# Row norms, rotary angles and adaLN sums in the first stage of a hybrid decoder block: other engines, another order

## The chip, the cores and the metric

One core of one Trainium2 chip runs the kernel, in float32. The core has TensorE (PE, matrix products into PSUM), VectorE (DVE), ScalarE (ACT, activation tables) and GpSimd (POOL), and a queue on SyncE (SP) that issues all the DMAs here. Each engine works through its own list of instructions in order and waits on semaphores for the others. The metric is the device time of one execution in microseconds, the median of several.

## The reference, cut to what matters

One decoder layer, 1024 positions of width 1024. Token mixing (two kinds of attention), then an MLP, each ahead with a modulated RMS norm. What the change touches is the norm ahead of the first projection, its modulation, and the rotary angles:

```python
def rms_norm(x, g):
    return x * rsqrt(mean(x * x, axis=-1, keepdims=True) + EPS) * g

ang = positions[..., None] * inv_freq            # 8 frequencies
cos, sin = jnp.cos(ang), jnp.sin(ang)
mod = silu(c) @ w_ada + b_ada                    # 6 vectors of 1024
sh_a, sc_a, gt_a, sh_m, sc_m, gt_m = split(mod, 6)
h = rms_norm(x, g_attn_pre) * (1 + sc_a) + sh_a
proj = h @ w_in                                  # 1024 x 2304, then attention
```

Behind it: rotary rotation of parts of `proj`, banded and dilated attention, an output projection, and `square(relu(h @ w_up)) @ w_down`.

## The kernel before, in words

A planner written in Python (class `Sched`) decides at build time in which order each engine gets its instructions. Every piece of work is an `op` with an engine (or a choice of engines), an estimated duration, what it depends on, buffers it takes and gives, a priority `prio` (lower goes first) and an urgency `crit`: `pick` takes the operation that can start first, unless one of higher `crit` can start within half its duration. What comes out is a fixed list for each engine; the estimates play no part when the kernel runs.

The first stage, up to some 60 us, computes `h` transposed and starts the first projection unit:

- x comes in eight blocks of 128 rows, `x_t[0]` to `x_t[7]`, in two halves of four. `x_block` squares and sums a block (`junk`, result in `ssq`; ScalarE L656 or VectorE L660), `rsqrt_mean` makes `rstd` of it (GpSimd: L484 adds EPS, L486 is a power of -0.5), and the block is scaled in place (`x_sb`; L676 on ScalarE, L677 on VectorE).
- `f_cond` makes silu(c) (`cond`) and a diagonal matrix of it (`diag`, L603). Two products with ones spread it over all partitions (`condb`, L614).
- `ada_chunk(k)`, for chunk k of 8 (128 channels each), has two sums over a tile `wa` of w_ada times `condb`, the scale `g_a` and the shift `s_a` (L687, a custom VectorE instruction with a read of its accumulator), and a small product (L691).
- `mod_chunk(k, half)`: four transposes into PSUM (`pxt`, L706), which need all four scaled blocks of the half; then ScalarE applies scale and shift twice, rounded to `hw` (L708, the high part) and whole to `h` (L714), and VectorE takes the difference as the low part (L717).
- `split_w` makes a high part (L560) and a low part (L565) of each piece of w_in. A product is then three matmuls, L909, L910 (high part of h) and L912 (low part).
- While TensorE has nothing to do, `filler` puts products of ones in its list (L926), up to the first product that uses the filler's own PSUM bank.
- The rotary angle is a product of position and frequency, brought into range by 2 x 2 rounding steps (L632, L633) and 12 parts of 2 pi that are subtracted (L635), then four closing steps (L639 to L642): 26 VectorE instructions of 128x64 (one of them L628), in groups of five, in `turn_steps`. Then two sines on ScalarE (`f_sin`, L649, L650), a negation (L731), and on GpSimd two sets of ten copies into rows (`tables`, L741, L747), which TensorE transposes (`ptab`, L753).

All loads go through SP in one order: x blocks 0 to 3, two tiles of w_ada, a piece of w_in, x blocks 4 to 7, then the rest in turn.

Of the kernel before, what the change touches and what calls it, by code (L numbers as in the profile page):

```python
# [189 lines left out]
class Sched:  # L190
# [162 lines left out]
def t_dv(n):  # L353
    return 0.066 + 0.00104 * n
# [19 lines left out]
def hybrid_block(ctx: ExitStack, tc: tile.TileContext, x, positions, w_mod, w_ada, b_ada, g_attn_post, w_in, w_out,  # L374
# [3 lines left out]
    V, A, G, T = nc.vector, nc.scalar, nc.gpsimd, nc.tensor  # L378
# [45 lines left out]
    ones = const.tile([P, P], F32, name="ones")  # L424
    nhalf = const.tile([P, KC], F32, name="nhalf")
# [10 lines left out]
    ssq = const.tile([P, TB], F32, name="ssq")  # L436
    rstd = const.tile([P, TB], F32, name="rstd")
# [18 lines left out]
    p0 = pool("p0", 1, "right", stack=right0)  # L456
# [20 lines left out]
    POOL_D1, POOL_D2 = (0.25, 0.65), (0.5, 1.2)  # L477

    def rsqrt_mean(dst, src, deps, dur):
        box, n = [], dst.shape[-1]  # L480

        def first():
            box.append(small.tile([P, 8], F32, name="rs_t", tag="rs_t"))
            G.tensor_scalar(box[0][:, 0:n], src, EPS, None, ALU.add)  # L484
        e = op("POOL", dur[0], first, deps, prio=0)
        return op("POOL", dur[1], lambda: G.tensor_tensor(dst, box[0][:, 0:n], nhalf[:, 0:n], ALU.pow), [e], prio=0)  # L486
# [7 lines left out]
    posf = p0.tile([P, TB], F32, name="posf")  # L494
# [9 lines left out]
    def r_in(a):  # L504
        return r_stg if a in beside else r_wa
# [20 lines left out]
    wa_t, wa_e = {}, {}  # L526
# [11 lines left out]
    x_t, x_e = {}, {}  # L538
# [55 lines left out]

    e_sin = op("ACT", 1.5, lambda: A.activation(small.tile([P, 8], F32, name="rs_t", tag="rs_t")[:, 0:1], ones[:, 0:1],
                                                AF.Sin), [e, e_init], prio=0)
# [9 lines left out]
    e = e_cond = op("DVE", 0.52 + t_dv(D), f_cond, [e], takes=[(r_wa, 1)], prio=0)  # L606
    e_condb = []
# [9 lines left out]
    def f_cols():  # L617
# [10 lines left out]
    turn_steps = [(0.22, lambda: V.tensor_tensor(ang[:], posf[:].unsqueeze(2).to_broadcast([P, TB, 8]),  # L628
                                                 inv_f.unsqueeze(1).to_broadcast([P, TB, 8]), ALU.mult))]

    def turns(inv, parts):
        turn_steps.append((0.2, lambda: V.tensor_scalar(kq[:], ang[:], inv, ROUND, ALU.mult, ALU.add)))  # L632
        turn_steps.append((0.2, lambda: V.tensor_scalar(kq[:], kq[:], -ROUND, None, ALU.add)))  # L633
        for part in parts:
            turn_steps.append((0.26, lambda part=part: V.scalar_tensor_tensor(ang[:], kq[:], -part, ang[:], ALU.mult,  # L635
                                                                              ALU.add)))
    turns(1.0 / (TWO_PI * 4096), COARSE)
    turns(1.0 / TWO_PI, FINE)
    turn_steps += [(0.2, lambda: V.tensor_scalar(ang[:], ang[:], 3.1415925, -3.1415925, ALU.min, ALU.max)),  # L639
                   (0.2, lambda: V.tensor_scalar(kq[:], ang[:], -1.0, None, ALU.mult)),  # L640
                   (0.22, lambda: V.tensor_tensor(kq[:], kq[:], ang[:], ALU.max)),
                   (0.2, lambda: V.tensor_scalar(kq[:], kq[:], -1.0, float(np.pi / 2), ALU.mult, ALU.add))]  # L642
# [8 lines left out]
    e_ang, e_xn = e, [[], []]  # L651

    def x_block(tb):
        def f_sq():
            junk = p0.tile([P, D], BF16, name="junk", tag="junk", bufs=2)
            A.activation(junk[:], x_t[tb][:], AF.Square, scale=1.0 / 32, accum_out=ssq[:, tb:tb + 1])  # L656

        def f_sq2():
            junk = p0.tile([P, D], BF16, name="junk", tag="junk", bufs=2)
            V.tensor_tensor_reduce(junk[:], x_t[tb][:], x_t[tb][:], 1.0 / D, 0.0, ALU.mult, ALU.add, ssq[:, tb:tb + 1])  # L660
        half = tb // 4
        e = op(("ACT", "DVE"), (1.25, 1.4), (f_sq, f_sq2), [x_e[tb]], prio=1 if half else -1)
        if half:
            pair.append((tb, e))
            if len(pair) < 2 and tb < 6:
                return
            tbs = [t for t, _ in pair]
            e = rsqrt_mean(rstd[:, tbs[0]:tbs[-1] + 1], ssq[:, tbs[0]:tbs[-1] + 1], [z for _, z in pair],
                           POOL_D2 if len(pair) > 1 else (0.3, 0.9))
            pair.clear()  # L670
        else:
            tbs = [tb]
            e = rsqrt_mean(rstd[:, tb:tb + 1], ssq[:, tb:tb + 1], [e], POOL_D1)
        for t in tbs:
            e_xn[half].append(op(("ACT", "DVE"), (1.15, 0.76),
                                 (lambda t=t: A.mul(x_t[t][:], x_t[t][:], rstd[:, t:t + 1]),  # L676
                                  lambda t=t: V.tensor_scalar(x_t[t][:], x_t[t][:], rstd[:, t:t + 1], None, ALU.mult)),  # L677
                                 [e], prio=-1))
    pair = []

    e_hh, e_hl, e_ada = {}, {}, {}

    def ada_chunk(k):

        def dot(i, dst):
            w = wa_t[k, i][:]
            V.tensor_tensor_reduce(w, w, condb[:], 1.0, bb[:, k, i:i + 1], ALU.mult, ALU.add, dst[:, k:k + 1])  # L687

        def f_g():
            dot(1, g_a)  # L690
            V.tensor_tensor(g_a[:, k:k + 1], g_a[:, k:k + 1], cols[:, 8 + k:9 + k], ALU.mult)  # L691
# [1742 lines left out]
```

## Time and profile before

| | us |
|---|---|
| median of three runs | 1099.63 (1098.22 to 2195.83) |
| the profiled execution's own time | 1098.02 |
| its span, first to last instruction | 1096.2 |
| mean granted TensorE clock in it | 0.998 |

"Span" is what the rows of the timeline are counted in; what lies around it is 1.8 us here. In a row of the timeline stand the start, the duration, the engine with the line, what is written and read, the shape, and in brackets how long the engine had been idle and who released it. A row of the stretches gives for each engine the busy time and the number of instructions; then the granted clock, the share of the DMA engines and GB/s. Rows of groups give a count, the sum and the mean in ns.

### The profile page before, as it was taken

How to read it: one execution, taken by the hardware profiler on the slowest of the kernel's cores; microseconds unless marked ns; L12 is line 12 of the kernel's file. 1: busy time of each engine (PE TensorE's matmuls, PEld its weight loads, DVE VectorE, ACT ScalarE, POOL GpSimd, SP SyncE). 2: the span in 40 equal slices, each digit the busy share in tenths (PEclk: the TensorE clock that was granted, in tenths of full speed). 3: DMA queues.
4: the chain of work that ended last, by engine and by line, in shares of the span. 5: the costliest groups of instructions: out<-in, count | busy, mean ns of one | idle time of the engine just before them, and what ended most of it. 6: DMA issues, size and time to landing. Idle time of an engine off the chain costs nothing.

```text
span 1096.2 us, 15266 instructions
## 1 busy us (share of the span) xinstructions
PE 1077.7 (98%) x5254; PEld 899.0 (82%) x5254; DVE 811.2 (74%) x1434; ACT 621.7 (57%) x1155; POOL 285.0 (26%) x378
## 2 busy tenths in 40 slices
PE   8999999999999999999999999999999999999996
PEld 6888888888888888888888888888888888888885
DVE  7968776766768687699796654897645995537998
ACT  6868876555556867686755244732245632337442
POOL 4649778596846531100000000000000000000002
PEclk9999999999999999999999999999999999999999
DMA  8565656454635457368711579231575043583104
GB/s 339 212 207 161 194 168 216 140 187 141 202 106 174 135 151 264 114 230 321 280 70 39 188 256 353 77 111 62 208 284 190 1 134 140 191 324 132 58 1 154
DMA packets 87230, 189.55 MB, mean 173 GB/s; under 512 B 8304, under 2 KB 24816, under 8 KB 87152
## 3 DMA queue, kind: packets, MB, share of 16 engines
q1 hardware_dynamic: 87152, 188.56, 49.6%
q8 instruction: 42, 0.69, 0.2%
q14 instruction: 36, 0.29, 0.1%
HBM read 139.25 MB, written 30.41 MB: 155 GB/s over the span
## 4 chain that ended last, share of the span: by engine, by line
PE 92%; DVE 4%; issue 1%; POOL 1%; ACT 1%; DMA 0%; DVEq 0%; POOLq 0%; SPq 0%
PE mlp_ps L2252 18%; PE mlp_ps L2250 18%; PE mlp_ps L2251 18%; PE pj L909 5%; PE pj L912 5%; PE pj L910 5%; PE y_ps L1815 3%; PE y_ps L1817 3%; PE y_ps L1816 3%; PE o_ps L1514 2%; PE s_ps L1323 1%; PE s_ps L1228 1%; PE o_ps L1415 1%; PE pt_ps L1380 1%; PE pt_ps L1479 1%
## 5 line engine op out<-in xcount | busy, mean ns | idle before, releaser
L2250 PE MATMUL mlp_ps<-hw 128*128 128x512 f32 x896 | 349.6, 390 | 0.0
L2252 PE MATMUL mlp_ps<-hw 128*128 128x512 f32 x896 | 348.6, 389 | 0.0
L2251 PE MATMUL mlp_ps<-hw 128*128 128x512 f32 x896 | 348.6, 389 | 0.0
L2251 PEld LDWEIGHTS mlp_ps<-hw 128*128 128x128 f32 x896 | 168.2, 188 | 35.3 <-issue 0.5
L2250 PEld LDWEIGHTS mlp_ps<-hw 128*128 128x128 f32 x896 | 168.2, 188 | 35.3 <-issue 0.5
L2252 PEld LDWEIGHTS mlp_ps<-hw 128*128 128x128 f32 x896 | 168.2, 188 | 34.9
L2017 DVE TENSOR_TENSOR hw<-w,hw 128x1024 fp32r<-128x1024 f32 x94 | 112.2, 1221 | 95.7 <-ACT hw L2010 93.0
L2010 ACT CAST hw<-w 128x1024 fp32r<-128x1024 f32 x94 | 95.7, 1050 | 129.8 <-PE mlp_ps L2252 94.5
L2350 POOL TENSOR_TENSOR st<-st,nhalf 128x1 f32<-128x1 f32 x8 | 7.8, 983 | 612.7 <-DVE st L2348 612.7
L909 PE MATMUL pj<-hw,w_hl 128*128 128x512 f32 x240 | 101.8, 424 | 0.0
L912 PE MATMUL pj<-hw,w_hl 128*128 128x512 f32 x240 | 94.5, 394 | 0.0
L910 PE MATMUL pj<-hw,w_hl 128*128 128x512 f32 x240 | 94.2, 392 | 0.0
L2010 ACT CAST hw<-u 128x1024 fp32r<-128x1024 f32 x48 | 48.7, 1053 | 64.5 <-PE mlp_ps L2252 64.5
L2017 DVE TENSOR_TENSOR hw<-u,hw 128x1024 fp32r<-128x1024 f32 x48 | 57.0, 1220 | 18.1 <-ACT hw L2010 18.1
L2308 DVE TENSOR_TENSOR yacc<-yacc,mlp_ps 128x512 f32<-128x512 f32 x96 | 62.2, 683 | 3.3 <-PE mlp_ps L2252 3.3
L1062 POOL TENSOR_TENSOR ada_acc<-ada_acc,wa_st 128x512 f32<-128x512 f32 x42 | 56.1, 1336 | 3.5
L912 PEld LDWEIGHTS pj<-hw,w_hl 128*128 128x128 f32 x240 | 45.0, 188 | 10.2
L1815 PE MATMUL y_ps<-hw,oh 128*128 128x512 f32 x128 | 51.6, 403 | 0.0
L1816 PE MATMUL y_ps<-hw,oh 128*128 128x512 f32 x128 | 50.0, 391 | 0.0
L909 PEld LDWEIGHTS pj<-hw,w_hl 128*128 128x128 f32 x240 | 45.4, 189 | 4.6
L910 PEld LDWEIGHTS pj<-hw,w_hl 128*128 128x128 f32 x240 | 45.5, 190 | 4.4
L2289 ACT ACTIVATE u<-u 128x512 f32<-128x512 f32 x48 | 29.0, 625 | 30.7 <-DVE u L2287 30.1
(259 smaller groups left out, 1988.3 us busy)
## 6 DMA issues: line engine op xcount, KB each, us to landing
hw<-s_dram SPq DMA_DIRECT2D x84, 512.0 KB, 4.1
wa_st<-in_w_ada SPq DMA_DIRECT2D x32, 512.0 KB, 4.5
w<-in_w_up SPq DMA_DIRECT2D x32, 512.0 KB, 4.7
w<-in_w_down SPq DMA_DIRECT2D x32, 512.0 KB, 6.8
s_dram<-hw SPq DMA_DIRECT2D x28, 512.0 KB, 3.2
qt<-hl SPq DMA_DIRECT2D x40, 256.0 KB, 2.5
w_st<-in_w_in SPq DMA_DIRECT2D x36, 256.0 KB, 3.0
x_sb<-in_x SPq DMA_DIRECT2D x16, 512.0 KB, 6.0
```

Of the source, the lines that this page charges most:

```text
L909: T.matmul(ps, w[:, 0, n], h[0], start=(k == 0), stop=False)
L910: T.matmul(ps, w[:, 1, n], h[0], start=False, stop=False)
L912: T.matmul(ps, w[:, 0, n], h[1], start=False, stop=(k == KC - 1))
L1062: G.tensor_tensor(ada.acc[:, :512], ada.acc[:, :512], wa[:, j], ALU.add)
L1815: T.matmul(ps[:], oh, wh[:, c0:c0 + 512], start=(k == 4 * m), stop=False)
L1816: T.matmul(ps[:], oh, wl[:, c0:c0 + 512], start=False, stop=False)
L2010: A.copy(out[j][0], flat(src[j]))
L2017: V.tensor_tensor(out[j][1], flat(src[j]), out[j][0].bitcast(F32), ALU.subtract)
L2250: T.matmul(ps[m][:], sh, mh, start=starts and k == 0, stop=False, **kw)
L2251: T.matmul(ps[m][:], sh, ml_, start=False, stop=False, **kw)
L2252: T.matmul(ps[m][:], sl, mh, start=False, stop=k == 3, **kw)
L2308: e = op("DVE", t_dv(512), lambda: V.tensor_tensor(y(), y(), ps[m][:], ALU.add), [e, ml.e_y[tb, n]], gives=gives, prio=1)
```

## The change

Roots. `rsqrt_mean` no longer uses GpSimd. ScalarE takes a square root of `ssq` + EPS (the constant tile `eps1`), and VectorE makes the reciprocal and one Newton step of it, four instructions of one column. It is done for each block by itself; before, two blocks of the second half shared one. So the table that ScalarE loads at the start is that of the square root (`e_root` for `e_sin`), and the sine's table is loaded when the sines come; they now wait for the evacuation of chunk 1, second half, and all scalings of the second half.

Angles. The steps of `turn_steps` up to the closing four go to GpSimd, one operation of the planner each; a subtraction of a part becomes two instructions (a product into `kp`, a sum). The closing four stay on VectorE, in one piece with `prio` -1 and `crit` 1.

Urgency. The two sums of chunk 0 get `crit` 3, the roots of the first half 2, its scalings 1. The negation of the sine has a higher priority and no longer waits for a low part of chunk 2.

```diff
-    def rsqrt_mean(dst, src, deps, dur):
...
-            G.tensor_scalar(box[0][:, 0:n], src, EPS, None, ALU.add)
-        e = op("POOL", dur[0], first, deps, prio=0)
-        return op("POOL", dur[1], lambda: G.tensor_tensor(dst, box[0][:, 0:n], nhalf[:, 0:n], ALU.pow), [e], prio=0)
+    def rsqrt_mean(dst, src, dep, crit):
+        r = small.tile([P, 8], F32, name="rs_x", tag="rs_x", bufs=TB)
+        e = op("ACT", 0.22, lambda: A.activation(r[:, 1:2], src, AF.Sqrt, bias=eps1[:]), [dep, e_root], prio=-2, crit=crit)
+
+        def f1():
+            a, y = r[:, 0:1], r[:, 1:2]
+            V.reciprocal(y, y)
+            V.scalar_tensor_tensor(a, src, EPS, y, ALU.add, ALU.mult)
+            V.scalar_tensor_tensor(a, a, -0.5, y, ALU.mult, ALU.mult)
+            V.scalar_tensor_tensor(dst, a, 1.5, y, ALU.add, ALU.mult)
+        return op("DVE", 0.62, f1, [e], prio=-2, crit=crit)
...
-        turn_steps.append((0.2, lambda: V.tensor_scalar(kq[:], ang[:], inv, ROUND, ALU.mult, ALU.add)))
-        turn_steps.append((0.2, lambda: V.tensor_scalar(kq[:], kq[:], -ROUND, None, ALU.add)))
+        turn_steps.append((0.2, lambda: G.tensor_scalar(kq[:], ang[:], inv, ROUND, ALU.mult, ALU.add)))
+        turn_steps.append((0.2, lambda: G.tensor_scalar(kq[:], kq[:], -ROUND, None, ALU.add)))
         for part in parts:
-            turn_steps.append((0.26, lambda part=part: V.scalar_tensor_tensor(ang[:], kq[:], -part, ang[:], ALU.mult,
-                                                                              ALU.add)))
+            turn_steps.append((0.25, lambda part=part: G.tensor_scalar(kp[:], kq[:], -part, None, ALU.mult)))
+            turn_steps.append((0.25, lambda: G.tensor_tensor(ang[:], kp[:], ang[:], ALU.add)))
...
-    for n in range(0, len(turn_steps), 5):
-        some = turn_steps[n:n + 5]
-        e = op("DVE", sum(z for z, _ in some), lambda some=some: [f() for _, f in some], [e, e_cond], prio=2)
+    for dur, f in turn_steps[:-4]:
+        e = op("POOL", dur + 0.1, f, [e, e_cond], prio=2)
+    e = op("DVE", 0.82, lambda: [f() for _, f in turn_steps[-4:]], [e], prio=-1, crit=1)
...
+        e = rsqrt_mean(rstd[:, tb:tb + 1], ssq[:, tb:tb + 1], e, 0 if half else 2)
...
-        eg = op("DVE", t_dv(D) + 0.25, f_g, [wa_e[k, 1], e_cols] + e_condb, gives=[(r_in((k, 1)), 1)], prio=1)
+        eg = op("DVE", t_dv(D) + 0.25, f_g, [wa_e[k, 1], e_cols] + e_condb, gives=[(r_in((k, 1)), 1)], prio=1,
+                crit=0 if k else 3)
...
-    e = op("ACT", 0.55, f_sin, [e_ang, e_sin], prio=1)
+    e = op("ACT", 1.85, f_sin, [e_ang, e_hh[1, 1]] + e_xn[1], prio=0)
...
-                [e, e_hl[2, 1]], prio=0)
+                [e], prio=-1)
```

What the planner makes of it shows at three places. First GpSimd, the end of its early work, before the rows of the rotary tables (`rows`); before:

```order
L484 TENSOR_SCALAR rs_t<-ssq 128x1
L486 TENSOR_TENSOR rstd<-rs_t,nhalf 128x1
L741 MEMSET rows 128x1024
L747 COPY rows<-cosw 128x8x8 x10
L741 MEMSET rows 128x1024
L747 COPY rows<-sinw 128x8x8 x10
```

And now:

```order
L639 TENSOR_SCALAR kp<-kq 128x64
L640 TENSOR_TENSOR ang<-kp,ang 128x64
L735 MEMSET rows 128x1024
L741 COPY rows<-cosw 128x8x8 x10
L735 MEMSET rows 128x1024
L741 COPY rows<-sinw 128x8x8 x10
```

The roots are gone; ahead of the rows stand 29 angle instructions, of which the last two are shown.

Second, VectorE between the two halves, from the low part of the first w_in piece on; before:

```order
L565 TENSOR_TENSOR w_hl<-w_st,w_hl 128x512
L660 ISA junk,ssq<-x_sb 128x1024
L660 ISA ssq 128x1
L717 TENSOR_TENSOR hw<-h,hw 128x4x128
L635 SCALAR_TENSOR_TENSOR ang<-kq,ang 128x64 x2
L639 TENSOR_SCALAR ang<-ang 128x64
L640 TENSOR_SCALAR kq<-ang 128x64
L641 TENSOR_TENSOR kq<-kq,ang 128x64
L642 TENSOR_SCALAR kq<-kq 128x64
L677 TENSOR_SCALAR x_sb<-x_sb,rstd 128x1024 x3
```

And now:

```order
L566 TENSOR_TENSOR w_hl<-w_st,w_hl 128x512
L664 ISA junk,ssq<-x_sb 128x1024
L664 ISA ssq 128x1
L643 TENSOR_SCALAR ang<-ang 128x64
L644 TENSOR_SCALAR kq<-ang 128x64
L645 TENSOR_TENSOR kq<-kq,ang 128x64
L646 TENSOR_SCALAR kq<-kq 128x64
L483 RECIPROCAL rs_x<-rs_x 128x1
L484 SCALAR_TENSOR_TENSOR rs_x<-ssq,rs_x 128x1
L485 SCALAR_TENSOR_TENSOR rs_x<-rs_x 128x1
L486 SCALAR_TENSOR_TENSOR rstd<-rs_x 128x1
```

The closing angle steps stand ahead of the second half's roots; behind the last row come a second root of four instructions, two scalings, the low part of chunk 0 (L711), two more roots and the third scaling. The low part of chunk 0 stood ahead of the angle steps before.

Third, the start of the second half. VectorE, from the last scaling on, before:

```order
L677 TENSOR_SCALAR x_sb<-x_sb,rstd 128x1024 x3
L687 ISA wa,g_a<-wa,condb,bb 128x1024
L687 ISA g_a 128x1
L691 TENSOR_TENSOR g_a<-g_a,head 128x1
L687 ISA wa,s_a<-wa,condb,bb 128x1024
L687 ISA s_a 128x1
L565 TENSOR_TENSOR w_hl<-w_st,w_hl 128x512
```

And now:

```order
L670 TENSOR_SCALAR x_sb<-x_sb,rstd 128x1024
L566 TENSOR_TENSOR w_hl<-w_st,w_hl 128x512
L680 ISA wa,g_a<-wa,condb,bb 128x1024
L680 ISA g_a 128x1
L684 TENSOR_TENSOR g_a<-g_a,head 128x1
L680 ISA wa,s_a<-wa,condb,bb 128x1024
L680 ISA s_a 128x1
L711 TENSOR_TENSOR hw<-h,hw 128x4x128
```

The second split has moved ahead of the sums of chunk 1. On TensorE, from the last high products of the first half to the second half's transposes, before:

```order
L909 MATMUL acc<-hw,w_hl 128x512
L910 MATMUL acc<-hw,w_hl 128x512
L912 MATMUL acc<-hw,w_hl 128x512 x3
L926 MATMUL acc<-ones_r 128x512 x17
L706 MATMUL pxt<-head,x_sb 128x128 x4
```

And now:

```order
L903 MATMUL acc<-hw,w_hl 128x512
L904 MATMUL acc<-hw,w_hl 128x512
L920 MATMUL acc<-ones_r 128x512 x9
L906 MATMUL acc<-hw,w_hl 128x512 x3
L920 MATMUL acc<-ones_r 128x512 x6
L700 MATMUL pxt<-head,x_sb 128x128 x4
```

Nine fillers now stand ahead of the low products (L906) and six behind them, where 17 stood behind them.

More of the change, by code (lines that the diff above doesn't have):

```diff
@@ L475, in load @@
         return op("SP", nbytes / (345e3 if prio > -500 else 370e3), emit, deps, takes=takes, prio=prio, gives=gives, after=after, n=n)
-    POOL_D1, POOL_D2 = (0.25, 0.65), (0.5, 1.2)
-    def rsqrt_mean(dst, src, deps, dur):
[L480 to L484, printed above, removed]
-        e = op("POOL", dur[0], first, deps, prio=0)
-        return op("POOL", dur[1], lambda: G.tensor_tensor(dst, box[0][:, 0:n], nhalf[:, 0:n], ALU.pow), [e], prio=0)
+    def rsqrt_mean(dst, src, dep, crit):
[8 more added lines that the diff above has]
+        return op("DVE", 0.62, f1, [e], prio=-2, crit=crit)
     FIRST = 8
@@ L584, in hybrid_block @@
     ones_r = p0.tile([P, 512], F32R, name="ones_r")
+    eps1 = p0.tile([P, 1], F32, name="eps1")
     fill = Tok()
@@ L591, in f_init @@
         V.memset(nhalf[:], -0.5)
+        V.memset(eps1[:], EPS)
     e_init = op("DVE", 0.4, f_init, prio=0)
     e = op("ACT", 0.1, lambda: A.activation(cond[:], c_raw, AF.Exp, scale=-1.0), [e_c], prio=0)
-    e_sin = op("ACT", 1.5, lambda: A.activation(small.tile([P, 8], F32, name="rs_t", tag="rs_t")[:, 0:1], ones[:, 0:1],
-                                                AF.Sin), [e, e_init], prio=0)
+    e_root = op("ACT", 1.5, lambda: A.activation(small.tile([P, 8], F32, name="rs_t", tag="rs_t")[:, 0:1], ones[:, 0:1],
+                                                AF.Sqrt), [e, e_init], prio=0)
     def f_cond():
@@ L626, in hybrid_block @@
     kq = p0.tile([P, TB, 8], F32, name="kq")
-    turn_steps = [(0.22, lambda: V.tensor_tensor(ang[:], posf[:].unsqueeze(2).to_broadcast([P, TB, 8]),
+    kp = p0.tile([P, TB, 8], F32, name="kp")
+    turn_steps = [(0.22, lambda: G.tensor_tensor(ang[:], posf[:].unsqueeze(2).to_broadcast([P, TB, 8]),
                                                  inv_f.unsqueeze(1).to_broadcast([P, TB, 8]), ALU.mult))]
     def turns(inv, parts):
-        turn_steps.append((0.2, lambda: V.tensor_scalar(kq[:], ang[:], inv, ROUND, ALU.mult, ALU.add)))
-        turn_steps.append((0.2, lambda: V.tensor_scalar(kq[:], kq[:], -ROUND, None, ALU.add)))
+        turn_steps.append((0.2, lambda: G.tensor_scalar(kq[:], ang[:], inv, ROUND, ALU.mult, ALU.add)))
+        turn_steps.append((0.2, lambda: G.tensor_scalar(kq[:], kq[:], -ROUND, None, ALU.add)))
         for part in parts:
-            turn_steps.append((0.26, lambda part=part: V.scalar_tensor_tensor(ang[:], kq[:], -part, ang[:], ALU.mult,
-                                                                              ALU.add)))
+            turn_steps.append((0.25, lambda part=part: G.tensor_scalar(kp[:], kq[:], -part, None, ALU.mult)))
+            turn_steps.append((0.25, lambda: G.tensor_tensor(ang[:], kp[:], ang[:], ALU.add)))
     turns(1.0 / (TWO_PI * 4096), COARSE)
@@ L662, in x_block @@
         e = op(("ACT", "DVE"), (1.25, 1.4), (f_sq, f_sq2), [x_e[tb]], prio=1 if half else -1)
[L663 to L679, printed above, removed]
+        e = rsqrt_mean(rstd[:, tb:tb + 1], ssq[:, tb:tb + 1], e, 0 if half else 2)
+        e_xn[half].append(op(("ACT", "DVE"), (1.15, 0.76),
+                             (lambda: A.mul(x_t[tb][:], x_t[tb][:], rstd[:, tb:tb + 1]),
+                              lambda: V.tensor_scalar(x_t[tb][:], x_t[tb][:], rstd[:, tb:tb + 1], None, ALU.mult)),
+                             [e], prio=-1, crit=0 if half else 1))
     e_hh, e_hl, e_ada = {}, {}, {}
@@ L691, in f_g @@
             V.tensor_tensor(g_a[:, k:k + 1], g_a[:, k:k + 1], cols[:, 8 + k:9 + k], ALU.mult)
-        eg = op("DVE", t_dv(D) + 0.25, f_g, [wa_e[k, 1], e_cols] + e_condb, gives=[(r_in((k, 1)), 1)], prio=1)
+        eg = op("DVE", t_dv(D) + 0.25, f_g, [wa_e[k, 1], e_cols] + e_condb, gives=[(r_in((k, 1)), 1)], prio=1,
+                crit=0 if k else 3)
         es = op("DVE", t_dv(D) + 0.16, lambda: dot(0, s_a), [wa_e[k, 0], e_cols] + e_condb,
-                gives=[(r_in((k, 0)), 1)], prio=1)
+                gives=[(r_in((k, 0)), 1)], prio=1, crit=0 if k else 3)
         e_ada[k] = [eg, es]
```

## The prediction

> **What bounds the kernel now.** I read the page's engine shares first, then the busy time in stretches of 10 us, then the timeline of the first 30 us.
>
> ```profile
> PE 1077.7 (98%) x5254; PEld 899.0 (82%) x5254; DVE 811.2 (74%) x1434; ACT 621.7 (57%) x1155; POOL 285.0 (26%) x378
> ```
> ```profile
> 10.00:20.00 10.00, 7.22 (x33) 5.46 (x32) 7.56 (x20) 8.03 (x13) 4.22 (x6) 1.00 1.03 413
> 20.00:30.00 10.00, 8.93 (x46) 6.97 (x45) 8.95 (x19) 7.11 (x14) 5.84 (x8) 1.00 0.77 299
> 30.00:40.00 10.00, 10.00 (x53) 8.33 (x52) 9.93 (x20) 9.12 (x15) 7.64 (x13) 1.00 0.80 294
> ```
>
> TensorE (PE) bounds the whole. From 30 us on it has no gap, and before that part of its work is filler. So the first stage is worth what it moves the moment from which TensorE has real work without a break. The path to that moment:
>
> ```profile
> 12.68 1.26 POOL L484 TENSOR_SCALAR rs_t<-ssq 128x1 f32<-128x1 f32 x1
> 14.02 1.66 POOL L486 TENSOR_TENSOR rstd<-rs_t,nhalf 128x1 f32<-128x1 f32 x1
> 15.71 1.15 ACT L676 ACTIVATE x_sb<-x_sb,rstd 128x1024 f32<-128x1024 f32 x1 [1.96 <-POOL rstd L486]
> 16.92 0.33 PE L706 MATMUL pxt<-head,x_sb 128*128 128x128 f32 x1 [2.78 <-ACT x_sb L676]
> 17.28 0.78 ACT L708 ACTIVATE hw<-pxt,s_a,g_a 128x512 fp32r<-128x512 f32 x1
> ...
> 23.49 1.51 POOL L486 TENSOR_TENSOR rstd<-rs_t,nhalf 128x1 f32<-128x1 f32 x1
> 24.68 1.28 DVE L687 CUSTOM_DVE_ANT_0 wa<-wa,condb,bb 128x1024 f32<-128x1024 f32 x1
> 25.03 1.15 ACT L676 ACTIVATE x_sb<-x_sb,rstd 128x1024 f32<-128x1024 f32 x1 [2.89 <-POOL rstd L486]
> 26.23 0.33 PE L706 MATMUL pxt<-head,x_sb 128*128 128x128 f32 x1 [1.07 <-ACT x_sb L676]
> ...
> 28.60 0.78 ACT L714 ACTIVATE h<-pxt,s_a,g_a 128x512 f32<-128x512 f32 x1
> 29.43 0.50 PE L909 MATMUL acc<-hw,w_hl 128*128 128x512 f32 x1
> ```
>
> Each half (four blocks of x) ends in a root on GpSimd (POOL), a scaling, and the transposes. The second half's transposes start at 26.23. The matmul at 29.43 waits for the evacuation of chunk 1, which needs the sums of w_ada that ended at 25.96; those were not late.
>
> **Why GpSimd is slow here.** The same copy costs 0.30 us alone and up to 1.33 us beside a busy VectorE (DVE):
>
> ```profile
> L747 POOL COPY rows<-cosw x8: 295/300/304, 123.2 to 124.4; 128x64 f32<-128x64 f32 x8
> ```
> ```profile
> L747 POOL COPY rows<-cosw x2: 769/1047/1325, 30.1 to 31.3; 128x64 f32<-128x64 f32 x2
> ```
> ```profile
> 30.02 1.28 DVE L687 CUSTOM_DVE_ANT_0 wa<-wa,condb,bb 128x1024 f32<-128x1024 f32 x1
> 31.23 0.72 DVE L717 TENSOR_TENSOR hw<-h,hw 128x512 fp32r<-128x512 f32 x1
> ```
>
> The copy that began at 30.1 ended 0.17 us after the 1.28 us sum, the next one 0.17 after the 0.72 us subtraction. Beside one large VectorE operation, one GpSimd instruction gets through.
>
> **The change, step by step.** The roots leave GpSimd, and 29 angle steps come in their place, each waiting for the one before: 1 product, 2 x 2 roundings, and 12 parts of two instructions, so 16 tensor-scalar and 13 tensor-tensor operations on 128x64.
>
> ```profile
> 5.42 1.22 DVE L603 TENSOR_TENSOR diag<-head,cond 128x1024 f32<-128x1024 f32 x1
> 7.34 0.24 POOL L484 TENSOR_SCALAR rs_t<-ssq 128x1 f32<-128x1 f32 x1 [6.91 <-ACT junk L656]
> 7.66 1.66 POOL L486 TENSOR_TENSOR rstd<-rs_t,nhalf 128x1 f32<-128x1 f32 x1
> 9.72 0.57 POOL L486 TENSOR_TENSOR rstd<-rs_t,nhalf 128x1 f32<-128x1 f32 x1
> 83.54 1.29 POOL L1062 TENSOR_TENSOR ada_acc<-ada_acc,wa_st 128x512 f32<-128x512 f32 x1
> ```
> ```profile
> L1355 POOL TENSOR_SCALAR p_sb<-p_sb,den 128x128 f32<-128x128 f32 x4 | 1.4, 373 | 0.8 <-DVE den L1347 0.8
> L1588 POOL TENSOR_TENSOR hw<-wo_st,hw 128x1024 fp32r<-128x1024 f32 x4 | 9.6, 2405 | 0.3
> ```
>
> A tensor-scalar step lies between 0.24 (1 column) and 0.37 (128): 0.30. A tensor-tensor step, on the line through 1.29 (512) and 2.41 (1024), is 0.31. Between two dependent ones lie 0.08 (7.58 to 7.66). So 0.39 a step, 11.4 in all from 6.7 (the end of `diag`): 18.1 if nothing holds it up. Then VectorE must run the last four angle steps, at a fixed place in its queue. When does it get there?
>
> ```profile
> 4.98 0.20 DVE L600 RECIPROCAL cond<-cond 128x8 f32<-128x8 f32 x1
> 7.93 0.59 ACT L614 COPY condb<-pbc 128x512 f32<-128x512 f32 x1 [0.68 <-PE pbc L611]
> 9.63 1.26 DVE L635 SCALAR_TENSOR_TENSOR ang<-kq,ang 128x64 f32<-128x64 f32 x5
> 10.80 0.75 DVE L677 TENSOR_SCALAR x_sb<-x_sb,rstd 128x1024 f32<-128x1024 f32 x1
> 13.90 0.16 DVE L691 TENSOR_TENSOR g_a<-g_a,head 128x1 f32<-128x1 f32 x1
> 17.41 0.69 DVE L565 TENSOR_TENSOR w_hl<-w_st,w_hl 128x512 fp32r<-128x512 f32 x1 [2.14 <-ACT w_hl L560]
> 18.01 1.22 DVE L660 CUSTOM_DVE_ANT_0 junk<-x_sb 128x1024 bf16<-128x1024 f32 x1
> 20.51 0.20 DVE L640 TENSOR_SCALAR kq<-ang 128x64 f32<-128x64 f32 x1
> 20.74 0.22 DVE L641 TENSOR_TENSOR kq<-kq,ang 128x64 f32<-128x64 f32 x1
> ```
>
> A small dependent VectorE instruction comes each 0.23. A Newton step (reciprocal 0.20, three like the 0.16 one, 0.03 between) is 0.8. Operations in a row start some 0.08 before the last one's end. From 8.5 (the first copy of `condb`) stand ahead of the angle steps: four Newton steps 3.2, three scalings 2.0, the two first sums and a product 2.6, a w_in split 0.6, a square 1.1. Arrival: 18.1.
>
> Seven of these are large (3 x 0.75, 2 x 1.28, 0.69, 1.22, together 6.7 us), and let one GpSimd step through each. In the other 4.7 us up to 18.1, 12 steps run. So 19 of 29 are done, and 10 x 0.39 = 3.9 us remain: VectorE waits until 22.0.
>
> Queued behind that wait is everything the second half needs: four steps 0.9 (22.9), two Newton steps (24.5), two scalings (25.8), the low part of chunk 0 (26.4), two Newton steps (28.0). ScalarE's (ACT) scaling takes 1.15, and the transposes start at 29.2, 3.0 later than before. The sums of chunk 1, no longer ahead of this, now follow a scaling and a split: 29.3, then 1.4 (a sum of 1.28 and its product of 0.16) and 1.3 to 32.0; two evacuations on ScalarE (0.7 and 0.78) free the bank at 33.4, and the matmul that ran at 29.43 runs at 33.5: **+4.1 us**. From there both engines were full before (10.00 and 9.93 of 10 in the row of 30 to 40), and the order on TensorE and SP behind the first stage is almost word for word the old one; so I expect the lag to be carried to the end, neither growing nor recovered.
>
> What I cost at nothing. First half: its third and fourth root end on VectorE at 15.7, the scaling at 16.4, against 16.86; but ScalarE squares a fifth block first (1.05), so its evacuation starts at 17.1 instead of 17.28. Eight roots (0.2 each) and one more square on ScalarE end near 22, long before it needs the last root at 28.0. The sine's table load moves from the idle start into the busy stretch:
>
> ```profile
> 4.71 1.28 ACT L595 ACT_TABLE_LOAD   x1
> 39.66 8.04 POOL L747 COPY rows<-sinw 128x64 f32<-128x64 f32 x10
> 59.57 0.60 PE L753 MATMUL ptab<-head,rows 128*128 128x128 f32 x4
> ```
>
> Behind two more evacuations and a split (33.4 + 0.7 + 0.8 + 0.5) it starts near 35.4 and the sines end near 37, while ScalarE's next chunk waits for sums that end near 37.7 (32.0, three low parts 1.8, two splits 1.2, 1.4 and 1.3), and VectorE's negation of the sine stands behind these sums; without that cover the load costs at most 1.3. SP's queue is in the same order.
>
> Bounds. A step as cheap as the bare copy (8 in 1.53 by their starts, 0.19, plus 0.08) leaves a wait of 1.2: +1.4 in all. Tensor-tensor steps as dear as the 0.57 power give 0.50 a step, a wait of 6.3, +6.5. Four Newton steps on the path at 0.7 or at 1.04 (four of the 0.26 steps) shift it by -0.4 or +1.0. I take the middle, since the rows nearest in kind and width lie there. Both ends together: +1.0 to +7.5.
>
> **The rivals.**
>
> *TensorE also falls to its slow rate.* Filler matmuls come 0.43 us apart at the start, later 0.23:
>
> ```profile
> L926 PE MATMUL acc<-ones_r x8: 628/628/795, 1.5 to 4.7; 128*128 128x512 f32 x8
> ```
> ```profile
> L926 PE MATMUL acc<-ones_r x15: 389/389/389, 9.7 to 12.9; 128*128 128x512 f32 x15
> ```
>
> An idle stretch of 2.78 us (to 16.92) did no harm. Now nine fillers end near 21.9, and the three matmuls behind them wait for the low part at 26.4: 4.5 us idle, longer than any seen before. If TensorE is slow after it, those three and six fillers take 9 x 0.43 = 3.9 instead of 2.1 and end at 30.3, past the transposes' 29.2: 1.1 more, +5.2, 1103.4. The Trainium skill, page "TensorE: Matmul & The Clock Gate", section "What's actually happening", states that the array falls to half rate after an idle window of about 3.4 us, the windows running freely; by that rule 4.5 us contain a whole window in some cases only, and the time would be 1102.3 or 1103.4. The trace shows no idle stretch long enough to test it.
>
> *GpSimd keeps pace* (the other side: not slower). If VectorE's large operations let these narrow steps pass, the angles end at 18.1, just as VectorE arrives; the 3.9 us go, and +0.2 remains: 1098.4. It decides at 18.1. Against it: the addition of 1.26 and the powers of 1.66 above were one column wide and were held up all the same.
>
> *The tables come late.* The rows on GpSimd now begin behind that negation and end near 56 (two sets of 8 us of copies and 1 us of clearing from 37.8) instead of 47.7. TensorE wants the sine rows at 59.57 + 4.1 = 63.7; 7 us of slack, unless copies take 12 us a set. Then each us more costs one: about 1104.
>
> **How the numbers follow.** The sum stands against the profiled execution's own 1098.0 (span 1096.2, 1.8 around it); the lowest run shown is 0.2 above that, the median 1.6. 1098.0 + 4.1 + 0.2 = 1102.3. Chances: forecast 0.62, slow rate 0.2, GpSimd keeps pace 0.1, tables late 0.03, something else 0.05. The bounds give 1099.2 to 1105.7, which also hold the slow rate; the 1098.4 of the kept pace is left out. With a little for the scatter of the runs: 1099.0 to 1106.0. Over 2% is 22 us, about what a measurement of this kernel can tell from no change, and several times any term here: faster 0.01, within 0.97, slower 0.02.
>
> **What would show it.** In the profile after: 29 small GpSimd instructions from 6.7 to about 22, stretched beside each large VectorE operation; VectorE idle some 4 us ahead of the last angle steps, released by GpSimd; transposes of the second half at 29 instead of 26.2; matmul durations of 0.39 (not 0.63) after TensorE's idle 4.5 us; nothing new after 60 us. The forecast is wrong if the angle steps end by 18, or if TensorE's steady stretch starts before 30.

## The result, and the profile after

| | before | after |
|---|---|---|
| median of all runs | 1098.09 us (6 runs) | 1102.97 us (6 runs) |
| profiled execution, its own time | 1098.02 us | 1101.48 us |
| first matmul of the first projection unit (`pj`) | 66.85 us | 70.13 us |

One run of each kernel took about twice as long (2195.83 and 2198.37 us) and is not in the ratio. The ratio is 1.0041 with a 95% interval of [1.0028, 1.0054], some 4.5 us slower. A second measurement, further down, gave 1.0028 [1.0015, 1.0041], some 3.1 us. By a bound of 2% that is no change; the forecast was 1102.3.

The busy time in stretches, of the kernel after (columns as in the rows of before):

```profile
20.00:30.00 10.00, 7.10 (x30) 5.40 (x28) 8.47 (x29) 3.90 (x10) 0.77 (x3) 0.83 0.71 275
30.00:40.00 10.00, 9.59 (x52) 7.87 (x50) 9.44 (x19) 9.88 (x17) 3.38 (x6) 1.00 0.87 313
```

TensorE lost 1.83 us of busy time between 20 and 30 us, although it ran slower there for a while: the granted clock was 0.83. Between 30 and 40 it has a gap that it did not have. So the loss lies where the forecast put it. GpSimd's part, from the timeline after:

```profile
3.51 0.29 POOL L632 TENSOR_TENSOR ang<-posf,head 128x64 f32<-128x64 f32 x1 [3.08 <-DMA head<-in_consts]
...
6.47 0.37 POOL L639 TENSOR_SCALAR kp<-kq 128x64 f32<-128x64 f32 x1
6.93 0.33 POOL L640 TENSOR_TENSOR ang<-kp,ang 128x64 f32<-128x64 f32 x1
7.34 0.37 POOL L639 TENSOR_SCALAR kp<-kq 128x64 f32<-128x64 f32 x1
...
13.38 1.35 POOL L639 TENSOR_SCALAR kp<-kq 128x64 f32<-128x64 f32 x1
14.81 0.35 POOL L640 TENSOR_TENSOR ang<-kp,ang 128x64 f32<-128x64 f32 x1
...
20.62 0.32 POOL L640 TENSOR_TENSOR ang<-kp,ang 128x64 f32<-128x64 f32 x1
```

The chain starts at 3.51, as soon as its data are there. Undisturbed, two steps take 0.87 (6.47 to 7.34), 0.43 each; beside a large VectorE operation one takes up to 1.35. Now VectorE and ScalarE in the same view:

```profile
18.52 0.08 DVE L664 DVE_READ_ACCUMULATOR2_ANT ssq<- 128x1 f32 x1
20.98 0.19 DVE L643 TENSOR_SCALAR ang<-ang 128x64 f32<-128x64 f32 x1 [2.39 <-POOL ang L640]
26.47 1.15 ACT L669 ACTIVATE x_sb<-x_sb,rstd 128x1024 f32<-128x1024 f32 x1 [4.40 <-DVE rstd L486]
```

VectorE stands for 2.39 us at the closing steps, released by GpSimd, and ScalarE waits behind it for the last root (4.40 idle). TensorE, timeline after:

```profile
20.08 2.20 PE L920 MATMUL acc<-ones_r 128*128 128x512 f32 x9
25.18 0.96 PE L906 MATMUL acc<-hw,w_hl 128*128 128x512 f32 x3 [2.90 <-DVE hw L711]
25.98 2.44 PE L920 MATMUL acc<-ones_r 128*128 128x512 f32 x6
28.22 1.05 PE L700 MATMUL pxt<-head,x_sb 128*128 128x128 f32 x4
32.68 0.50 PE L903 MATMUL acc<-hw,w_hl 128*128 128x512 f32 x1 [0.41 <-ACT h L708]
...
70.13 0.39 PE L903 MATMUL pj<-hw,w_hl 128*128 128x512 f32 x1
```

The nine fillers run out, TensorE is idle for 2.90 us, and then six fillers take 2.44 us, where six take 1.54 at full clock (run 2 below). The transposes of the second half start at 28.22, 2.0 us later than the last one before, which had waited for the last scaling (26.23; three of its four had run at 24.67). The matmul of chunk 1 comes 3.25 later (29.43 before), the first `pj` matmul 3.28 later. In the timeline before it stands at:

```profile
66.85 0.39 PE L909 MATMUL pj<-hw,w_hl 128*128 128x512 f32 x1
```

That one is the landmark used below: from it on TensorE is nearly full in both kernels (busy for 1016.46 of the 1029 us from 67 on before, for 1019.73 after). The slower stretch shows in the granted clock, by stretches after:

```profile
25.20:26.40 1.20, 1.20 (x5) 1.02 (x6) 0.99 (x8) 0.00 (x0) 0.00 (x0) 0.98 0.53 212
26.40:28.10 1.70, 1.70 (x5) 1.22 (x5) 1.70 (x4) 1.15 (x1) 0.00 (x0) 0.50 0.01 2
28.10:29.80 1.70, 1.70 (x8) 1.39 (x7) 1.67 (x4) 0.48 (x1) 0.00 (x0) 0.51 0.54 183
```

Half the clock for 3.4 us (26.4 to 29.8), beginning 1.2 us after the work came back.

### The profile page after: what moved, and what is told of

Read it like the earlier page. It is cut to its first block, busy times and chain, and to the rows that moved or that the text cites. A ratio compares the mean times of both kernels' runs of the same rounds, so it can differ in the third digit from the quotient of the medians.

```text
span 1099.7 us, 15307 instructions
## 1 busy us (share of the span) xinstructions
PE 1080.8 (98%) x5259; PEld 901.3 (82%) x5259; DVE 813.3 (74%) x1450; ACT 624.2 (57%) x1164; POOL 289.3 (26%) x393
## 4 chain that ended last, share of the span: by engine, by line
PE 92%; DVE 3%; POOL 2%; issue 1%; ACT 1%; DMA 0%; DVEq 0%; POOLq 0%; SPq 0%
PE mlp_ps L2245 18%; PE mlp_ps L2246 18%; PE mlp_ps L2244 18%; PE pj L903 5%; PE pj L906 5%; PE pj L904 5%; PE y_ps L1809 3%; PE y_ps L1811 3%; PE y_ps L1810 3%; PE o_ps L1508 2%; PE s_ps L1222 1%; PE s_ps L1317 1%; PE o_ps L1409 1%; PE pt_ps L1374 1%; PE acc L906 1%
## 5 line engine op out<-in xcount | busy, mean ns | idle before, releaser
L906 PE MATMUL pj<-hw,w_hl 128*128 128x512 f32 x240 | 94.4, 394 | 0.0
L2011 DVE TENSOR_TENSOR hw<-u,hw 128x1024 fp32r<-128x1024 f32 x48 | 56.9, 1218 | 18.1 <-ACT hw L2004 18.1
L906 PEld LDWEIGHTS pj<-hw,w_hl 128*128 128x128 f32 x240 | 45.0, 188 | 10.2
```

The costliest lines, as they stand in the source:

```text
L906: T.matmul(ps, w[:, 0, n], h[1], start=False, stop=(k == KC - 1))
L2011: V.tensor_tensor(out[j][1], flat(src[j]), out[j][0].bitcast(F32), ALU.subtract)
```

## The experiments

Two controls first, since their scatter is the scale for the rest: both kernels once more, unchanged.

> The kernel before once more, unchanged, profiled beside the variants. Question: several variants lose a further 0.9 to 1.3 us near 193, where TensorE waits for q_far behind a GpSimd product whose w_ada tile lands late; the first profile of the kernel before has no such wait. Theory (the landing time of that tile scatters from run to run and from chip to chip): this profile shows the wait too, or a landing at another distance from the first pj matmul than the 117.1 us of the first profile (183.9 less 66.85). Rival (the changed order brings the wait): again no idle time of TensorE over 0.3 between 185 and 200, landing at 184 within 0.3. Both: first pj matmul 66.3 to 67.3, ratio 0.999 to 1.001.

> The changed kernel once more, unchanged, on the same chip. VectorE waits 2.0 to 2.8 us for the angles, till 20.9 to 21.5; TensorE idle 2.8 to 3.4 us ahead of the low-part products; first pj matmul 69.8 to 70.8; ratio 1.003 to 1.005. If the slow TensorE rate is set by where its idle time falls against a window that runs on its own, the slow stretch may be absent or at another distance from the idle time than 1.2 us; if by the length of the idle time alone, it is there again and alike.

Measured: before against itself 1.0008 [0.9996, 1.0019]; after 1.0028 [1.0015, 1.0041]. The timeline of before, second profile:

```profile
28.62 0.51 PE L909 MATMUL acc<-hw,w_hl 128*128 128x512 f32 x1
...
66.02 0.39 PE L909 MATMUL pj<-hw,w_hl 128*128 128x512 f32 x1
...
191.08 1.19 PE L1228 MATMUL s_ps<-kt,q_far 128*128 128x128 f32 x8 [0.63 <-POOL q_far L1204]
```

The timeline of after, second profile:

```profile
20.82 0.20 DVE L643 TENSOR_SCALAR ang<-ang 128x64 f32<-128x64 f32 x1 [1.93 <-POOL ang L640]
25.02 0.96 PE L906 MATMUL acc<-hw,w_hl 128*128 128x512 f32 x3 [2.39 <-DVE hw L711]
27.20 0.65 PE L700 MATMUL pxt<-head,x_sb 128*128 128x128 f32 x4
31.74 0.50 PE L903 MATMUL acc<-hw,w_hl 128*128 128x512 f32 x1 [0.93 <-ACT h L708]
...
69.36 0.39 PE L903 MATMUL pj<-hw,w_hl 128*128 128x512 f32 x1
```

Three readings. The landmark of one kernel scatters by 0.8 (66.85 and 66.02; 70.13 and 69.36). The distance between the kernels is 3.28 in the first pair of profiles and 3.34 in the second; taken crosswise it is 2.51 to 4.11, so a landmark of one profile is good to about 0.8. The wait for `q_far` near 191, which several variants show, is in the kernel before as well; the change does not bring it. And in this profile of after TensorE was idle for 2.39 us and kept its clock, yet the loss at the landmark is the same: the half clock is no needed part of it.

**1. Is it the wait for GpSimd?** The chain cut short, nothing moved:

```diff
-        for part in parts:
+        for i, part in enumerate(parts):
+            if i:
+                turn_steps.extend([(0.25, lambda: None)] * 2)
+                continue
```

> The order of all other instructions is that of the changed kernel; of the twelve parts of 2 pi only the first coarse and the first fine one are subtracted, the other ten (20 GpSimd instructions) are left out, so GpSimd has 9 angle steps instead of 29. Theory (the wait of VectorE for the angle steps, and the slow TensorE rate that its idle time sets off, are the cost): the steps end by 12 us, VectorE runs the closing steps without a wait near 18.6, TensorE is idle for under 1 us ahead of the second half's low-part products, its matmuls come 0.23 apart and not 0.43 there, the second half's transposes start near 25.2 instead of 28.2, the first pj matmul near 66.9 instead of 70.1, and the time falls by about 3.3 us against the changed kernel: ratio to before 1.000 to 1.002. Rival (the Newton steps on VectorE and the later sums of chunk 1 are the cost): the transposes still start after 27.5 and the time stays within 1 us of the changed kernel's, ratio 1.003 to 1.005.

Measured: 1.0005 [0.9992, 1.0019]. Timeline of this run:

```profile
18.88 0.19 DVE L646 TENSOR_SCALAR ang<-ang 128x64 f32<-128x64 f32 x1
...
25.28 0.63 PE L703 MATMUL pxt<-head,x_sb 128*128 128x128 f32 x4
29.80 0.50 PE L906 MATMUL acc<-hw,w_hl 128*128 128x512 f32 x1 [0.95 <-ACT h L711]
...
67.46 0.39 PE L906 MATMUL pj<-hw,w_hl 128*128 128x512 f32 x1
```

No wait, the transposes at 25.28, the landmark 1.9 to 2.7 earlier than after. The rival falls. But the landmark is still 0.6 to 1.4 later than before's, so the wait is most of the loss and not all.

**2. What does the half clock cost?** More fillers in TensorE's idle time:

```diff
-        for _ in range(n):
+        for _ in range(n + 13 if n == 9 else n):
```

> The changed kernel with 22 instead of 9 filler matmuls ahead of the second half's low-part products, about 3 us more of work for TensorE that nobody reads, in the time in which it was idle for 2.90 us. Theory (after the idle time TensorE runs at about half rate for 3 us, and that delays the second half's transposes by 0.6 and the rest by 0.9): no matmul there comes 0.43 apart any more, the transposes start near 27.6, the first pj matmul near 69.2, and the time falls by 0.9 us: ratio to before about 1.0032. Rival (the slow rate is hidden behind the scaling on ScalarE that ends at 27.6, or comes back elsewhere): the first pj matmul stays within 0.3 of 70.1 and the time within 0.4 us.

Measured: 1.0042 [1.0026, 1.0059]. Timeline of this run:

```profile
21.43 0.20 DVE L643 TENSOR_SCALAR ang<-ang 128x64 f32<-128x64 f32 x1 [2.79 <-POOL ang L640]
...
26.43 1.54 PE L920 MATMUL acc<-ones_r 128*128 128x512 f32 x6
27.81 0.65 PE L700 MATMUL pxt<-head,x_sb 128*128 128x128 f32 x4
32.35 0.50 PE L903 MATMUL acc<-hw,w_hl 128*128 128x512 f32 x1 [0.96 <-ACT h L708]
...
69.96 0.39 PE L903 MATMUL pj<-hw,w_hl 128*128 128x512 f32 x1
```

Six fillers take 1.54 again, but the time did not fall, and by the landmark alone the rival was right. The angles came 0.45 later in this run, though: their chain started at 4.15 instead of 3.51, for the constants landed later. From the closing steps to the landmark it is 48.5 us here (69.96 - 21.43) and 48.5 in the second profile of after, both at full clock, against 49.15 in the first, with the half clock. So it costs about 0.6, not 0.9; the rest hides in the wait for chunk 1's evacuation, which is longer without it (0.96 and 0.93 against 0.41).

**3. Does VectorE's delay at this place go through?** The angle steps on VectorE, all in one piece:

```diff
-        e = op("POOL", dur + 0.1, f, [e, e_cond], prio=2)
-    e = op("DVE", 0.82, lambda: [f() for _, f in turn_steps[-4:]], [e], prio=-1, crit=1)
+        e = op("POOL", dur + 0.1, lambda: None, [e, e_cond], prio=2)
+    e = op("DVE", 0.82, lambda: [f() for f in on_v] + [f() for _, f in turn_steps[-4:]], [e], prio=-1, crit=1)
```

> The order is that of the changed kernel, but the angle steps ahead of the closing four run on VectorE, one after the other, at the place of the closing steps (25 more VectorE instructions, no GpSimd ones). They take 25 x 0.23 = 5.9 us, where the changed kernel waited for 2.4. Theory (what VectorE does or waits at this place delays the second half by the same amount): closing steps at 24.5 instead of 21.0, transposes near 31.5, first pj matmul near 73.6, time 3.5 us above the changed kernel's, ratio to before about 1.007. Rival (VectorE has slack behind this place, and the start of the steady TensorE work is set by something else): within 1 us of the changed kernel.

Measured: 1.0054 [1.0038, 1.0071]. The expectation counted wrongly: VectorE subtracts a part in one instruction, so there are 17 ahead of the closing four, not 25 (and 21 in the kernel before, not the 26 of the section on it). Timeline of this run:

```profile
18.20 0.22 DVE L644 TENSOR_TENSOR ang<-posf,head 128x64 f32<-128x64 f32 x1
22.48 0.20 DVE L651 TENSOR_SCALAR ang<-ang 128x64 f32<-128x64 f32 x1
...
26.68 1.65 PE L914 MATMUL acc<-hw,w_hl 128*128 128x512 f32 x3 [4.52 <-DVE hw L719]
```

They take 4.28 us. The closing steps run 1.50 later than in the first profile of after and 1.66 later than in the second, and the landmark (71.83) 1.70 and 2.47 later. VectorE has no slack behind this place.

**4. The closing steps out of the way, by the planner or by hand.** First its estimate of a GpSimd step raised, so that it orders anew:

```diff
-        e = op("POOL", dur + 0.1, f, [e, e_cond], prio=2)
+        e = op("POOL", dur + 0.35, f, [e, e_cond], prio=2)
```

> The changed kernel, but the planner counts each GpSimd angle step 0.25 us longer (about 0.6 instead of 0.35; 0.43 was measured without disturbance). It then puts the closing angle steps on VectorE behind the second half's scalings and the second chunk's low part, and the sines later too. All work is the same. Theory: VectorE does not wait for GpSimd ahead of the second half, the transposes start near 25.5, the first pj matmul near 67, time 3 us below the changed kernel's, ratio to before 0.999 to 1.002. Rival (the sums of chunk 1 or the Newton steps hold the second half up): transposes after 27, ratio above 1.003. A second rival (the sines come too late for the tables): the matmul of ptab waits, the first pj matmul comes no earlier than 69.

Measured: 1.0037 [1.0024, 1.0051], landmark 69.65. Timeline of this run, TensorE and then VectorE:

```profile
22.54 0.27 PE L700 MATMUL pxt<-head,x_sb 128*128 128x128 f32 x1
...
23.88 0.33 PE L700 MATMUL pxt<-head,x_sb 128*128 128x128 f32 x1 [0.22 <-DVE x_sb L670]
...
31.25 0.50 PE L903 MATMUL acc<-hw,w_hl 128*128 128x512 f32 x1 [3.63 <-ACT h L708]
```
```profile
25.77 1.28 DVE L680 CUSTOM_DVE_ANT_0 wa<-wa,condb,bb 128x1024 f32<-128x1024 f32 x1
27.17 0.69 DVE L711 TENSOR_TENSOR hw<-h,hw 128x512 fp32r<-128x512 f32 x1
27.77 0.68 DVE L566 TENSOR_TENSOR w_hl<-w_st,w_hl 128x512 fp32r<-128x512 f32 x1
28.37 1.28 DVE L680 CUSTOM_DVE_ANT_0 wa<-wa,condb,bb 128x1024 f32<-128x1024 f32 x1
```

VectorE no longer waits and the last transpose for the first chunk of the second half comes at 23.88, 2.3 us earlier than in the first profile of before, and nothing is won: the planner put a low part and a split between the two sums of chunk 1, the second ended at 29.65, and TensorE stood 3.63 us for it. The expected 3 us did not come. The rival with the sums was right for this order: its ratio above 1.003 came, though its transposes after 27 did not. The second rival had the landmark right (no earlier than 69), but not the reason: TensorE does not wait at `ptab` in this run. Then the closing steps moved by hand, and everything else left in its order:

```diff
-    e = op("DVE", 0.82, lambda: [f() for _, f in turn_steps[-4:]], [e], prio=-1, crit=1)
+    e = op("DVE", 0.82, lambda: None, [e], prio=-1, crit=1)
...
-        es = op("DVE", t_dv(D) + 0.16, lambda: dot(0, s_a),
+        es = op("DVE", t_dv(D) + 0.16, lambda: [dot(0, s_a)] + [f() for _, f in turn_steps[-4:] if k == 1],
```

> The changed kernel with all its work and its order, but the four closing angle steps on VectorE stand behind the shift sum of chunk 1 instead of ahead of the second half's Newton steps. Theory (the wait for GpSimd is the whole cost): no wait of VectorE at its old place (18.5) nor at the new one (27), TensorE idle for under 1 us ahead of the low-part products, no slow TensorE rate, transposes of the second half near 24.8 instead of 28.2, matmul of chunk 1 near 28.8 instead of 32.7, first pj matmul between 66.0 and 67.0 (changed kernel 70.1, before 66.85), ratio to before 0.999 to 1.001. Rival (the closing steps only wait or delay at the new place instead, and with them the low part of chunk 1, the sums of chunk 2 and the rotary tables): first pj matmul after 68.5.

Measured: 1.0022 [1.0013, 1.0032]; no wait for GpSimd at either place, transposes at 24.32. Timeline of this run:

```profile
28.86 0.50 PE L903 MATMUL acc<-hw,w_hl 128*128 128x512 f32 x1 [0.96 <-ACT h L708]
...
67.29 0.39 PE L903 MATMUL pj<-hw,w_hl 128*128 128x512 f32 x1
```

All the work is done, so this is the change without its wait: 2.1 to 2.8 better than after by the landmark, and still 0.4 to 1.3 behind before. The landmark was expected at 66.0 to 67.0 and the ratio at no more than 1.001, so the wait is not the whole cost.

**5. What is the rest?** It is not lost ahead of the matmul of chunk 1: 28.86 lies between the two profiles of before (29.43 and 28.62). It is lost behind it: from there to the landmark 38.43 us pass, where 37.4 to 37.7 pass in before, in after and in runs 1 to 3. The closing steps, 0.82 us on VectorE (27.18 to 28.00), now stand ahead of the low part of chunk 1 and the sums of chunk 2, and from 25 to 44 us VectorE has no gap of over 0.05 us. Their size fits; no run took them away from there. In run 1, where they stand ahead, the matmul of chunk 1 itself was 0.4 to 1.2 later than before instead (29.80). So VectorE is short of time at either place, and the next two runs take work from it: it got eight Newton steps for the 17 angle steps it lost. The second half's roots in pairs, on top of the last run:

```diff
-            a, y = r[:, 0:1], r[:, 1:2]
+            if tb % n != n - 1:
+                return
+            a, y, src, dst = r[:, 0:n], r[:, 2:2 + n], ssq[:, first:first + n], rstd[:, first:first + n]
```

> The kernel with the closing steps behind the shift sum of chunk 1 (the run above), and in the second half one Newton step of two columns for two blocks instead of two of one column: 8 VectorE instructions of some 0.19 us less. Theory (VectorE's own work, the Newton steps among it, sets when chunk 1's sums end): matmul of chunk 1 0.6 to 1.5 us earlier than in the run above, first pj matmul between 65.0 and 66.2, ratio 0.997 to 1.000, the first version ahead of the kernel before. Rival (ScalarE's squares and its scaling set it, not VectorE): matmul of chunk 1 within 0.3 us of the run above.

Then, on top of that, only the reciprocal:

```diff
-            V.reciprocal(y, y)
-            V.scalar_tensor_tensor(a, src, EPS, y, ALU.add, ALU.mult)
-            V.scalar_tensor_tensor(a, a, -0.5, y, ALU.mult, ALU.mult)
-            V.scalar_tensor_tensor(dst, a, 1.5, y, ALU.add, ALU.mult)
+            V.reciprocal(dst, y)
```

> The kernel of the pairs (closing steps behind the shift sum of chunk 1, second half's roots in pairs) with the Newton step left out: VectorE makes only the reciprocal of ScalarE's root, one instruction instead of four, so the roots keep the error of ScalarE's table. Theory (VectorE's Newton instructions take what the moved angle steps had freed): 3 x 0.19 us less at each of six places, 1.1 of it in the second half; second half's transposes 0.5 to 1 us earlier than with pairs (23.98), first pj matmul 65.2 to 66.0, ratio 0.5 to 1 thousandth under that of the pairs (1.0016). Rival (VectorE's work is no longer the bound there; ScalarE's squares and roots, or the DMAs, are): first pj matmul within 0.3 of 66.4.

Measured: pairs 1.0016 [1.0006, 1.0027], landmark 66.37; without Newton 1.0003 [0.9991, 1.0015], landmark 65.86. The matmul of chunk 1 in the first and in the second of these, each from its timeline:

```profile
27.98 0.50 PE L911 MATMUL acc<-hw,w_hl 128*128 128x512 f32 x1 [0.46 <-ACT h L716]
```
```profile
27.46 0.50 PE L908 MATMUL acc<-hw,w_hl 128*128 128x512 f32 x1 [0.46 <-ACT h L713]
```

Each removal of VectorE work moves it and the landmark by about the same (28.86, 27.98, 27.46; 67.29, 66.37, 65.86); the 38.4 us between them stay. The steps are about as large as the scatter of a landmark, but they follow the order expected, and the matmul moved by the size expected. With pairs the landmark just missed the expected 65.0 to 66.2, and that kernel is not ahead of before, though the theory expected it to be. The intervals of the three ratios overlap, so the times alone don't tell them apart. No version here is faster than before.

**6. One part alone.** The angles moved and the roots left on GpSimd: the kernel before, with the angle steps' part of the diff and nothing else of it.

> The kernel before with the move of the angle steps to GpSimd alone: roots on GpSimd, urgency and tables as before. The planner puts the GpSimd roots between the angle steps, and the closing steps on VectorE behind both sums of chunk 1 and all scalings. Theory (the angle steps leave VectorE 4.3 us of work less, of which the Newton steps in the changed kernel use 6.2 again): no long wait of VectorE for the angles, the second half's transposes between 24.5 and 26.5, first pj matmul between 65.3 and 67.3, ratio 0.998 to 1.001. Rival (a root on GpSimd now waits behind angle steps that are held up beside large VectorE operations, 0.4 to 1.3 us each, two times in a row): first half's last transposes after 18.5 instead of 16.9, first pj matmul after 68.5, ratio above 1.002.

Measured: 1.0069 [1.0056, 1.0082], landmark 73.29, the slowest of all. GpSimd, then ScalarE and TensorE, in the timeline of this run:

```profile
13.55 1.60 POOL L486 TENSOR_TENSOR rstd<-rs_t,nhalf 128x1 f32<-128x1 f32 x1
...
27.04 1.60 POOL L486 TENSOR_TENSOR rstd<-rs_t,nhalf 128x1 f32<-128x1 f32 x1
```
```profile
28.68 1.15 ACT L677 ACTIVATE x_sb<-x_sb,rstd 128x1024 f32<-128x1024 f32 x1 [2.64 <-POOL rstd L486]
...
30.72 0.33 PE L707 MATMUL pxt<-head,x_sb 128*128 128x128 f32 x1 [0.51 <-DVE x_sb L678]
```

The theory failed here: the last transposes of the second half come at 30.72 instead of 26.23, for the roots queue behind angle steps that are themselves held up. The rival has the place right for the second half; in the first it named 18.5, and the last one came at 17.62. Part of the 73.29 is also two stretches of half clock (17.5 to 20.9 and 31.2 to 34.6); what they cost here was not measured apart. So in this order the roots and the angles get in each other's way on GpSimd. The roots moved without the angles were not tried. Last, the urgency of chunk 0's sums taken back:

```diff
-                crit=0 if k else 3)
+                crit=0)
```

> The changed kernel without the urgency of chunk 0's two sums (the planner then puts them behind the scalings of the first half and the first split, and one square of the second half behind the closing steps). Theory: the first product of the first half comes some 1.5 to 2.5 us later, where TensorE only has fillers otherwise; VectorE still waits for the angles, till about 21, and has 1.3 us more to do after it, so the matmul of chunk 1 and the first pj matmul come 0 to 1 us later than in the changed kernel: pj 70.1 to 71.2, ratio 1.003 to 1.006. Rival (the urgency itself displaced the second half's work and is part of the loss): pj before 69.3, ratio under 1.003.

Measured: 1.0036 [1.0024, 1.0048], landmark 70.00. The first product of the first half comes at 20.00 instead of 18.12, VectorE waits 1.93 for the angles, and the landmark lies between the two of after (70.13 and 69.36), just under the expected 70.1 to 71.2. The urgency neither helped nor hurt by more than the scatter.

## Why the forecast held, point by point

- *TensorE bounds; the first stage is worth what it moves, 1:1 to the end.* Right in the first pair of profiles: 3.28 at the landmark and 3.47 us in their times. In the second pair it is 3.34 and 2.47. What lies behind the landmark scatters by more than that difference (1029.35 and 1031.98 us of the span in the two profiles of before), so the runs show 1:1 only within some 2 us.
- *GpSimd's chain, 0.39 a step from 6.7, the end of `diag`.* Wrong in two sizes that cancel in part. The chain needs only the constants and the positions and started at 3.51; that it follows `diag` is in the planner's list of dependences, not in the data. And a free step takes 0.43.
- *One step gets through beside each large VectorE operation, 10 left when VectorE arrives.* Right in kind: 1.20 and 1.35 beside the two first sums. VectorE arrived at 18.6 (forecast 18.1) with the twenty-fourth step running and five behind it, so the wait was 2.39, not 3.9.
- *The wait delays all of the second half, +4.1.* Right in mechanism (runs 1, 3 and the second of 4); +3.25 measured at the matmul of chunk 1. The term that was too large is the wait, by 1.5. Of that, 0.5 is only VectorE's later arrival; the closing steps began 1.0 earlier than forecast (20.98 against 22.0). From there to the matmul of chunk 1 the sum has 11.5: it took 11.70 with the half clock, and 10.92 without it in the second profile and in run 2.
- *The sums of chunk 1 then stand behind the second half's roots, scaling and split.* Right: with the wait gone, the matmul of chunk 1 still follows VectorE's work ahead of it (28.86, 27.98, 27.46 as Newton instructions go). What the forecast did not have is how full VectorE is behind that: moving the closing steps there left the landmark 0.9 behind the mean of before (67.29 against 66.4), lost behind the matmul of chunk 1, and leaving out Newton instructions made up for it.
- *First half, sine table and tables at nothing.* Right: the first evacuation at 17.31, the table load at 34.49 (forecast 35.4), and TensorE waits 0.36 us for the tables, as long as before.
- *Rival: slow rate.* Half right. It came in one profile of two, after an idle time of 2.90, shorter than the 4.5 it was tied to, and cost 0.6, not 1.1. The Trainium skill, page "TensorE: Matmul & The Clock Gate", section "What's actually happening", has windows of 3413 ns that run freely; the trace agrees with the length (3.4) and with a start that is not tied to the work. It also says "after ≥1 idle window", and there the trace differs: the idle time of 2.90 is shorter than a whole window, and in the 3.4 us ahead of the drop TensorE was busy for 1.22.
- *Rival: GpSimd keeps pace.* It did not: VectorE waited in both profiles.
- *The number.* That 1102.3 lies so near the median of 1102.97 is partly luck. The first stage lost 3.3 us and not 4.1, and the second measurement puts the whole at some 3.1.

## What to carry to other kernels

Moving work to an idle engine makes a chain of it there: price one dependent step including the gap, and count how many of its steps meet a large VectorE operation, before putting what closes the chain at a fixed place in a busy engine's queue. Behind such a place look for what is late next: here the shift sum of a chunk mattered as much as the transposes, and transposes 2.3 us earlier were worth nothing without it. Compare kernels by a landmark in the trace, with the same kernel profiled twice, when a difference is a few thousandths.

## What the runs showed of the hardware

The half clock came in pieces of 3.4 us, and which idle time sets it off is not told by its length. The idle times in the first stage: 2.90 (after, first profile), 4.52 (angles on VectorE), 3.63 (raised estimate) and 2.19 (angles alone) were followed by it; 2.78 (before), 2.39 (after, second profile) and 1.76 (no urgency) were not. With the angles alone another piece began at 17.5, after 1.57 us of idle time, 0.3 of work, and within the next idle time. Only with the angles on VectorE was TensorE idle for the whole 3.4 us ahead of the drop; in the other cases of the first stage it was busy for 0.76 to 1.22 of them. In the kernel before, second profile, it fell on a place far behind, where TensorE had mainly narrow matmuls; by stretches:

```profile
382.80:386.20 3.40, 2.29 (x15) 1.58 (x14) 2.80 (x8) 2.70 (x6) 1.49 (x4) 1.00 0.20 49
386.20:389.60 3.40, 3.40 (x14) 2.97 (x14) 2.48 (x5) 0.59 (x1) 3.40 (x4) 0.51 1.04 349
```

TensorE was busy for 2.29 of the 3.4 us ahead of it. That execution has a span of 1098.0 against 1096.2, although its landmark came 0.83 earlier. Such a piece, hit or missed, is a likely reason why runs of one kernel differ by one or two us. Of the 67 executions of before measured beside the experiments, the 15 with a mean clock of 0.998 took 1098.06 us in the median, the 8 with 0.994 took 1100.90; and run 1's profile, the longest of its twelve executions (1103.35), has two such pieces behind the landmark, from 195.3 and from 390. That is an association, not a trial, and how much activity it takes to be spared was not tried.
